# Expert loop in program order on four engines, memory rows loaded late, router logits partly inside the last projection

## The chip, the cores and the metric

The kernel runs on one core of one Trainium2 chip. The metric is the device time in microseconds (us) of one execution. Five instruction streams matter: PE (TensorE, matmuls and transposes), DVE (VectorE), ACT (ScalarE), POOL (GpSimd) and SP (SyncE, which issues nearly all loads and stores). Each runs its own instructions in the order in which they stand and stops at the first whose inputs are not there.

## What is computed

Two transformer blocks on 512 tokens of 1024 features, in fp32. The first block ends in a hierarchical mixture of experts, which is the part that the change touches:

```
x = x + einsum('bsd,de->bse', y, w_out)              # "last projection" of the first block: x1
h2 = rmsnorm(x, norm_ffn_g).reshape(b * s, d)
group_logits = h @ w_router_group + b                 # 8 groups
g_sel = argmax(group_logits)                          # one group for each token
in_group = (h @ w_router_expert + b)[its group]       # 4 experts
top_vals, top_idx = top_k(in_group, 2)                # two of them
for e in range(32):
    hid = silu(h @ w_gate[e]) * (h @ w_up[e])         # 1024 -> 256
    out = out + (hid @ w_down[e]) * combine[:, e]     # 256 -> 1024
```

The second block has two layers: A (dilated windows) and B, and in both the tokens also attend to a second input of 512 "memory" rows. The memory's keys and values for both layers need only those rows and weights, so the kernel computes them beside the experts and uses them as filling work for PE.

## The kernel before, in words

**Weights.** A `Stream` object (L195 on) loads all big weights in a planned order on SP, as far ahead as the buffer rings of its "lanes" allow. A tile of 128x1024 fp32 is 512 KB. Tiles of the lane "w" are split after landing into two fp32r parts, `whi` on ACT (L229) and `wlo` on DVE or, for every eighth, on POOL (L232), and used in products of three matmuls (L370 to L372). Expert weights are used as they land, without a split. Each call of `ws.get()` also pushes loads and splits ahead (`advance`), so splits of weights that come later in the plan are emitted wherever the loop happens to take an expert tile.

**Router.** After the last projection (L1120s), x1 is transposed (L1119), the logits are made with the router's weights as the stationary side, 64 columns by 512 tokens (L1160), copied out (`lT`) and turned back by four transposing matmuls (L1177). Then DVE picks group and experts, PE counts positions (L1242, `ppos`), DVE forms slot ranks, PE forms the slot table (L1338), and `v0i` holds, for each slot, the row to gather. Steps of the memory's keys and values (`pump(kv, n)`) fill PE in between.

**Experts.** The 32 experts are handled as 16 pairs, 64 slots for each of the two. For pair j, POOL gathers 128 rows of x1 from HBM with an indirect DMA into `xg` (L1377, two buffers), DVE scales them (L1380), PE transposes them in 8 steps (L1385), DVE copies them out (`xgt`, L1387); PE multiplies by gate and up in four units (L1400), ACT and DVE form the hidden values (L1405 to L1407), PE turns them (L1413), ACT copies (`hid`, L1415), PE multiplies by down (L1426), ACT and DVE copy `y` (L1430, L1428), and POOL scatters it to HBM by an indirect DMA (`yd`, L1431). The loop at L1462 stands in this order in the program:

```
for j in range(-1, 16):
    hidden(j); gate_up(j+1) units 0 to 2; tokens(j+2): gather and transposes
    turned(j); gate_up(j+1) unit 3; down(j) and scatter
```

A scheduler orders the instructions of each engine, except inside `tc.manual_schedule(engines=...)`, where the named engines keep the program's order. Before, only PE is named in the router and in the loop. At j == 8 the loop also loads the memory rows for layer B's values into `mem` and splits them (`mem_load`, L635 on ACT, L636 on DVE).

**After the loop.** `vB_steps` and `mem_k` (memory work of layer B and more) run on PE while SP reads `yd` back and DVE adds it to x2 (`add_experts`, L1553, L1554); squares for two norms follow, then the transposes and layer A's first projection.

Of the kernel before, what the change touches and what calls it, by code (L numbers as in the profile page):

```python
# [195 lines left out]
class Stream:  # L196
# [3 lines left out]
    def __init__(self, nc, plan, ahead):  # L200
        self.nc, self.plan, self.ahead = nc, plan, ahead
        self.lanes, self.count, self.raw, self.done, self.pos = {}, {}, [], [], 0
# [75 lines left out]
ROUTER = (1, 1, 1, 2, 4, 4, 8)  # L278
AFTER = (5, 3, 3, 3, 1)
# [30 lines left out]
def build(tc, A, out, dbg=None):  # L310
# [259 lines left out]
    plan2 = [(ap, "k" if 8 <= j < 12 else "w") for j, ap in enumerate(plan2)]  # L570
    ws = Stream(nc, [(ap, "w") for ap in plan1 + kv0] + moe_u + plan2, ahead=3)
    ws.lane("w", wp, "wraw", 3, "w", 5, pool_every=8)
    ws.lane("k", wp, "wraw", 3, "w", 5, pool_every=1)
# [31 lines left out]
    def outproj(yT, xs, view, after=None):  # L605
# [4 lines left out]
        for n in range(2):  # L610
            pp = [acc(), acc(), scp(), scp()]
            for u in range(nk // 2):
                hi, lo = ws.get()
                for c in range(4):
# [13 lines left out]
    def mem_load(pool):  # L628

        res = []  # L630
        for j in range(2):
            t = pool.tile([128, 1024], F32, name="mem", tag="mraw", bufs=MR)
            nc.sync.dma_start(t, mTd[:, 1024 * j:1024 * j + 1024])
# [456 lines left out]
    wr = big("wr", "y", 2)[:, :512].rearrange("p (k n) -> p k n", k=8)  # L1090
    G.memset(wr, 0.0)
    nc.sync.dma_start(wr[:, :, :40], A["w_r"])
    V.tensor_tensor(wr, wr, vec(V_FFN, 8)[:, :, None].to_broadcast([128, 8, 64]), OP.mult)
    ident2 = mo.tile([128, 40], F32, name="ident2")
    V.tensor_tensor(ident2, ident[:, :40], ident[:, 64:104], OP.add)
# [10 lines left out]

    def square_half(pool, junk):
# [34 lines left out]
    outproj(yT, x1, xv, after_x1)  # L1142
# [10 lines left out]
    order = ExitStack()  # L1153
    order.enter_context(tc.manual_schedule(engines={mybir.EngineType.PE}))
    plT = otp()

    def logits(k):
        for kk in (k, k + 1):
            q = slice(64 * (kk % 2), 64 * (kk % 2) + 64)
            T.matmul(plT[q], wr[:, kk, :], x1T[kk], start=kk < 2, stop=kk > 5)  # L1160
    logits(0)
    logits(2)
    x1_transpose(4)
    x1_transpose(5)
    pump(kv, ROUTER[0])
    x1_transpose(6)
    pump(kv, ROUTER[1])
    x1_transpose(7)
    logits(4)
    pump(kv, ROUTER[2])  # L1170
    logits(6)
    lT = mo.tile([128, 512], F32, name="lT", tag="mkn", bufs=2)
    V.tensor_copy(lT, plT)
    pump(kv, ROUTER[3])
    pl = otp()
    for c in range(4):
        T.matmul(pl[:, c * 40:c * 40 + 40], lT[:, c * 128:c * 128 + 128], ident2, start=True, stop=True)  # L1177
    pump(kv, ROUTER[4])

# [9 lines left out]
    def small(shape, name, dtype=F32, tag=None, rows=128):
        return mo.tile([rows] + shape, dtype, name=name, tag=tag or name)  # L1190

    def bc(ap, shape):
        return ap.to_broadcast([128] + shape)
# [19 lines left out]
    basei = [small([4, 5], "basei%d" % z, BF) for z in range(2)]  # L1213
    for z in range(2):
        for i in range(4):
            V.memset(basei[z][:, i, 0:1], float(4 * z + i + 1))
    iop = small([1], "iop")
    junkp = mo.tile([128, 512], F32, name="junkp", tag="mkn", bufs=2)[:, :128]
    V.scalar_tensor_tensor(junkp, ident, 1.0, iota, op0=OP.mult, op1=OP.mult, accum_out=iop)
    for z in range(2):  # L1220
        V.tensor_copy(basei[z][:, :, 1], iop.to_broadcast([128, 4]))
    revi = small([8], "revi")
    V.tensor_scalar(revi, iota[:, :8], -1.0, 8.0, OP.mult, OP.add)
# [9 lines left out]
    sel = [small([4, 8, 4], "sel%d" % z, BF) for z in range(2)]  # L1233
    for z, o in enumerate((o1, o2)):
        V.tensor_tensor(sel[z], bc(oh[:, :, :, None], [4, 8, 4]), bc(o[:, :, None, :], [4, 8, 4]), OP.mult)
    both = small([4, 32], "both", BF)
    flat = [z.rearrange("p c g e -> p c (g e)") for z in sel]
    V.tensor_tensor(both, flat[0], flat[1], OP.add)
    ppos = otp()
# [5 lines left out]
    pump(kv, ROUTER[5])  # L1245
# [54 lines left out]
    def three(dst, src, n):  # L1300
        for z in range(3):
            V.tensor_copy(dst[:, :, n * z:n * z + n], src)
            if z < 2:
                V.tensor_tensor(src, src, dst[:, :, n * z:n * z + n], OP.subtract)

    def payload(base, z, n, name):
        p = small([4, 32, n], name, BF)
        V.tensor_tensor(p, bc(base[:, :, None, :], [4, 32, n]), bc(flat[z][:, :, :, None], [4, 32, n]), OP.mult)
        return p

    r1 = small([4, 1], "r1")
    V.tensor_copy(r1[:, :, 0], r[:, :4])
    three(basei[0][:, :, 2:5], r1, 1)
    V.tensor_copy(basei[1][:, :, 2:5], basei[0][:, :, 2:5])
    payi = [payload(basei[z], z, 5, "payi%d" % z) for z in range(2)]

    def slot_ranks(shift, name):
# [3 lines left out]
        for z in range(2):  # L1321
# [5 lines left out]
            for i in range(4):  # L1327
                V.tensor_scalar(R[:, i, :], iota[:, :NS], pr[:, i:i + 1], None, OP.is_equal)
# [16 lines left out]
    def slot_rows(t, n, name):  # L1345
# [10 lines left out]
        V.tensor_tensor(ix, f, e, OP.add)  # L1356
        w = small([n], name + "w")
        V.tensor_tensor(w, t[:, :, 4], t[:, :, 3], OP.add)
        V.tensor_tensor(w, w, t[:, :, 2], OP.add)
        return ix, ox, w  # L1360

    def slot_weights(t, n, name):
# [3 lines left out]
        V.tensor_tensor(w, w, t[:, :, 0], OP.add)  # L1366
        return w

    ranks = slot_ranks(None, "s0")
    idx, odx, rw = slot_rows(slot_table(ranks, payi, 5, "ti"), 16, "v0")  # L1370
    pump(kv, ROUTER[6])
    order.close()

    def gather_tokens(j, ix, rms):
# [5 lines left out]
        V.tensor_scalar(xg, xg, rms, None, OP.mult)  # L1380
# [21 lines left out]
    def hidden(p, w):  # L1402

        th = hchunk("th")[:, :256]
        S.activation(th, p[:, :256], AF.Tanh, scale=0.5)  # L1405
# [30 lines left out]
    Xg = gather_tokens(0, idx[:, 0:1], rw[:, 0:1])  # L1436
    pump(kv, 32 - sum(ROUTER))
    basew = [small([4, 3], "basew%d" % z, BF) for z in range(2)]
    payw = []
    for z, w in enumerate(top_weights()):  # L1440
        three(basew[z], w[:, :, None], 1)
        payw.append(payload(basew[z], z, 3, "payw%d" % z))
    cw = slot_weights(slot_table(ranks, payw, 3, "tw"), 16, "cw")
    nx, ofs, next_i = counts()

# [7 lines left out]
    def tokens(j):  # L1453
        return gather_tokens(j, idx[:, j:j + 1], rw[:, j:j + 1])

    order = ExitStack()
    order.enter_context(tc.manual_schedule(engines={mybir.EngineType.PE}))
    pg, Xnext = acc(), None
    for j in range(-1, 16):
        if j >= 0:  # L1460
            th = hidden(pg, cw[:, j:j + 1])
# [26 lines left out]
    def extra(e):  # L1488
# [36 lines left out]
        down(get, turned(hidden(p, w[:, 0:1])), ox)  # L1525
# [14 lines left out]
    ET = mybir.EngineType  # L1540
    with tc.manual_schedule(engines={ET.PE, ET.Activation, ET.DVE, ET.Pool}):
        kmB = [mo.tile([128, 512], F32, name="kmB", tag="mraw", bufs=MR) for _ in range(2)]
        ms, ms2 = ([big("m", "mraw", MR) for c in range(4)] for _ in range(2))
        for c in range(4):
            nc.sync.dma_start(ms[c], yd[128 * c:128 * c + 128, :])
            nc.sync.dma_start(ms2[c], yd[512 + 128 * c:640 + 128 * c, :])
        pump(vB_steps)
# [3 lines left out]
        def add_experts(c):  # L1551
            pump(kv, AFTER[c])
            V.tensor_tensor(x2[c], x2[c], ms[c], OP.add)  # L1553
            V.tensor_tensor(x2[c], x2[c], ms2[c], OP.add)  # L1554
            tap("x2", x2[c], c)
            S.activation(ms[c], x2[c], AF.Square, accum_out=s3[:, c:c + 1])
        hT = transposed(x2, gFA, hp_, "h", 16, tps=tps, more=scp, before=add_experts)
        for c in range(4):
            m = ms[c]
# [501 lines left out]
```

## Time and profile before

| | us |
|---|---|
| median of 3 runs | 1874.06 |
| lowest, highest run | 1872.5, 1877.54 |
| profiled execution | 1873.42 |
| its span in the trace | 1871.6 |
| PE busy in it | 1791.2 (96%) |
| DVE, ACT, POOL busy | 894.3, 733.9, 368.0 |
| mean granted PE clock, as a share of full speed | 0.984 |

The span is what the trace covers; 1.8 us of the profiled execution lie around it. Times within the trace count from the span's start. The router takes the stretch from 447 to 489, the expert loop that from 489 to 741, and the work up to layer A's first projection that from 741 to 778. PE's busy share is an average over all stages.

### The profile page before, as it was taken

How to read it: one execution, taken by the hardware profiler on the slowest of the kernel's cores; microseconds unless marked ns; L12 is line 12 of the kernel's file. 1: busy time of each engine (PE TensorE's matmuls, PEld its weight loads, DVE VectorE, ACT ScalarE, POOL GpSimd, SP SyncE). 2: the span in 40 equal slices, each digit the busy share in tenths (PEclk: the TensorE clock that was granted, in tenths of full speed). 3: DMA queues.
4: the chain of work that ended last, by engine and by line, in shares of the span. 5: the costliest groups of instructions: out<-in, count | busy, mean ns of one | idle time of the engine just before them, and what ended most of it. 6: DMA issues, size and time to landing. Idle time of an engine off the chain costs nothing.

```text
span 1871.6 us, 25322 instructions
## 1 busy us (share of the span) xinstructions
PE 1791.2 (96%) x9426; PEld 1381.5 (74%) x9426; DVE 894.3 (48%) x1880; ACT 733.9 (39%) x1754; POOL 368.0 (20%) x463
## 2 busy tenths in 40 slices
PE   8999999998999578999999999999999999999999
PEld 8857776786533123799989899989888787777887
DVE  4389765276422221742342422342475326676571
ACT  5475355343100011544554433553564332333460
POOL 1301200010111011413514203514200002222200
PEclk9999999999999789999999999999999999999999
DMA  5221222178899998642211222212233322121231
GB/s 179 79 68 35 73 68 74 58 248 316 327 414 409 413 396 312 231 132 90 91 59 55 68 90 90 79 54 71 68 113 110 117 90 80 57 68 57 68 113 57
DMA packets 83684, 261.16 MB, mean 140 GB/s; under 512 B 12896, under 2 KB 14688, under 8 KB 83552
## 3 DMA queue, kind: packets, MB, share of 16 engines
q1 hardware_dynamic: 78080, 248.43, 37.6%
q0 software_dynamic: 4608, 8.40, 1.2%
q10 hardware_dynamic: 864, 2.62, 0.4%
q8 instruction: 77, 1.26, 0.3%
q14 instruction: 55, 0.45, 0.1%
HBM read 248.92 MB, written 18.87 MB: 143 GB/s over the span
## 4 chain that ended last, share of the span: by engine, by line
PE 85%; DMA 9%; DVE 3%; ACT 2%; issue 1%; SPq 0%; POOL 0%; POOLq 0%; ACTq 0%; DVEq 0%
PE acc L370 19%; PE acc L372 18%; PE acc L371 18%; PE acc L1400 3%; PE sc L370 3%; PE sc L371 3%; PE sc L372 3%; DMA mraw<-in_w_moe 3%; DMA hraw<-in_w_moe 2%; PE sc L1931 1%; PE sc L1426 1%; PE sc L911 1%; PE sc L1727 1%; DMA xraw<-in_w_moe 1%; PE tp L1668 1%; PE oT L936 1%
## 5 line engine op out<-in xcount | busy, mean ns | idle before, releaser
L370 PE MATMUL acc<-whi,hh 128*128 128x512 f32 (+2 forms) x936 | 382.5, 410 | 1.4 <-ACT hh L383 0.6
L371 PE MATMUL acc<-wlo,hh 128*128 128x512 f32 (+2 forms) x936 | 372.1, 398 | 0.0
L372 PE MATMUL acc<-whi,hl 128*128 128x512 f32 (+2 forms) x936 | 371.6, 399 | 0.0
L232 DVE TENSOR_TENSOR wlo<-wraw,whi 128x1024 fp32r<-128x1024 f32 (+4 forms) x209 | 244.6, 1174 | 254.0 <-ACT whi L229 253.3
L229 ACT ACTIVATE whi<-wraw 128x1024 fp32r<-128x1024 f32 (+4 forms) x239 | 239.2, 1002 | 294.2 <-PE acc L371 114.8
L370 PEld LDWEIGHTS acc<-whi,hh 128*128 128x128 f32 x936 | 223.1, 239 | 27.5 <-issue 2.8
L371 PEld LDWEIGHTS acc<-wlo,hh 128*128 128x128 f32 x936 | 223.8, 239 | 22.0 <-issue 1.7
L372 PEld LDWEIGHTS acc<-whi,hl 128*128 128x128 f32 x936 | 222.8, 239 | 21.5
L370 PE MATMUL acc<-hh,whi 128*128 128x512 f32 x448 | 184.7, 412 | 0.0
L372 PE MATMUL acc<-hh,wlo 128*128 128x512 f32 x448 | 177.7, 397 | 0.0
L371 PE MATMUL acc<-hl,whi 128*128 128x512 f32 x448 | 176.8, 395 | 0.0
L232 POOL TENSOR_TENSOR wlo<-wraw,whi 128x1024 fp32r<-128x1024 f32 (+3 forms) x30 | 69.1, 2304 | 514.9 <-ACT whi L229 423.9
L365 POOL TENSOR_TENSOR rs<-rsa,mhalf 128x4 f32<-128x4 f32 (+1 forms) x80 | 79.2, 990 | 333.2 <-DVE rsa L362 269.5
L707 ACT ACTIVATE hjk<-acc 128x128 bf16<-128x128 f32 x232 | 64.0, 276 | 106.6 <-PE acc L372 75.5
L370 PEld LDWEIGHTS acc<-hh,whi 128*128 128x128 f32 x448 | 84.5, 189 | 21.1 <-issue 4.9
L372 PEld LDWEIGHTS acc<-hh,wlo 128*128 128x128 f32 x448 | 84.2, 188 | 19.8 <-issue 1.0
L371 PEld LDWEIGHTS acc<-hl,whi 128*128 128x128 f32 x448 | 84.6, 189 | 15.5
L1400 PE MATMUL acc<-mraw,xgt 128*64 128x512 f32 x232 | 95.5, 621 | 0.3 <-DVE xgt L1387 0.3
L710 DVE TENSOR_TENSOR nat<-acc,rs 128x512 f32<-128x512 f32 x52 | 35.9, 691 | 61.2 <-POOL rs L365 43.4
L371 PE MATMUL sc<-wlo,hh 128*128 128x512 f32 (+2 forms) x144 | 56.0, 390 | 0.0
L370 PE MATMUL sc<-whi,hh 128*128 128x512 f32 (+2 forms) x144 | 55.7, 392 | 0.0
L372 PE MATMUL sc<-whi,hl 128*128 128x512 f32 (+2 forms) x144 | 55.0, 388 | 0.0
(546 smaller groups left out, 3084.7 us busy)
## 6 DMA issues: line engine op xcount, KB each, us to landing
mraw<-in_w_moe SPq DMA_DIRECT2D x86, 512.0 KB
wraw<-in_w_qka SPq DMA_DIRECT2D x48, 512.0 KB
xraw<-in_w_moe SPq DMA_DIRECT2D x25, 512.0 KB
hraw<-in_w_moe SPq DMA_DIRECT2D x44, 256.0 KB
praw<-in_w_moe SPq DMA_DIRECT2D x22, 512.0 KB
qraw<-in_w_moe SPq DMA_DIRECT2D x21, 512.0 KB
wraw<-in_w_va SPq DMA_DIRECT2D x20, 512.0 KB
wraw<-in_w_qfb SPq DMA_DIRECT2D x16, 512.0 KB
```

What stands on the lines that cost most here:

```text
L229: nc.scalar.activation(hi, raw, AF.Copy)
L232: eng.tensor_tensor(lo, raw, hi.bitcast(F32), OP.subtract)
L365: G.tensor_tensor(r[:, :m], t[:, :m], mhalf[:, :m], OP.pow)
L370: T.matmul(p, a[0], b[0], start=start, stop=False)
L371: T.matmul(p, a[0], b[1], start=False, stop=False)
L372: T.matmul(p, a[1], b[0], start=False, stop=stop)
L707: S.activation(jk, p[:, h * 128:h * 128 + 128], AF.Square, accum_out=st[:, h:h + 1])
L710: V.tensor_tensor(t.rearrange("p (h d) -> p h d", h=nh), p.rearrange("p (h d) -> p h d", h=nh), r[:, :nh, None].to_broadcast([128, nh, 128 ...
L911: T.matmul(pp[s][:, :W], a[:, i * 128:i * 128 + 128], b[:, :W], start=True, stop=True)
L936: T.matmul(o[64 * s:64 * s + 64, j * 128:512], vt[j][:, (2 * pr + s) * 64:(2 * pr + s) * 64 + 64], PT[pr, s][:, col[j]:col[j] + w], start= ...
L1400: T.matmul(p[z], X[2 * u + k][:, z], w[e][k], start=u + k == 0, stop=u + k == 4)
L1426: T.matmul(p[z], t[:, k * 128 + NS * e:k * 128 + NS * e + NS], w[e][k], start=k == 0, stop=k == 1)
```

## The change

1. **Router.** The logits are made with the transposed tokens as the stationary side, 128 tokens by 40 columns, in 32 matmuls (L1167 of the changed kernel) straight into the layout that DVE reads; `lT` and the four turning matmuls go. The half that needs only the first four transposed blocks stands inside the last unit of the last projection. DVE joins PE in keeping the program's order there. The payload products move from DVE to POOL, and four instructions for each slot rank become one. The filling steps are dealt out anew.
2. **Gathered rows** are no longer scaled by DVE; the norm's factor goes into the tanh's scale and the slot weights.
3. **Loop.** PE, ACT, DVE and POOL all keep the program's order, and a new limit `ws.upto` keeps splits of later weights out of it until j == 14.
4. **Memory rows** are loaded at j == 13 and split behind the loop (`mem_split`, L641, L642).
5. **After the loop** two of the adds stand between the memory steps, the second norm's square uses a precomputed gF squared, and one lane, which split four value weights on POOL alone, goes.

```diff
-            if not moved and d < i:
+            if not moved and d < i and (self.upto is None or d < self.upto):
...
-ROUTER = (1, 1, 1, 2, 4, 4, 8)
+ROUTER = (1, 1, 2, 9, 3)
...
-    plan2 = [(ap, "k" if 8 <= j < 12 else "w") for j, ap in enumerate(plan2)]
-    ws.lane("k", wp, "wraw", 3, "w", 5, pool_every=1)
...
+    def logits(k):
+        for kk in (k, k + 1):
+            for c in range(4):
+                T.matmul(pl[:, c * 40:c * 40 + 40], x1T[kk][:, run(c)], wr[:, kk, :], start=kk + c == 0,
+                         stop=kk == 7 and c == 3)
+    def early_logits():
+        logits(0)
+        logits(2)
+    outproj(yT, x1, xv, after_x1, early_logits)
...
-    for c in range(4):
-        T.matmul(pl[:, c * 40:c * 40 + 40], lT[:, c * 128:c * 128 + 128], ident2, start=True, stop=True)
...
-        V.tensor_scalar(xg, xg, rms, None, OP.mult)
...
-        S.activation(th, p[:, :256], AF.Tanh, scale=0.5)
+        S.activation(th, p[:, :256], AF.Tanh, scale=hr)
...
-    order.enter_context(tc.manual_schedule(engines={mybir.EngineType.PE}))
+    order.enter_context(tc.manual_schedule(engines={ET.PE, ET.Activation, ET.DVE, ET.Pool}))
+    own = len(plan1) + 8 + 192
+    ws.upto = own
...
-        if j == 8:
-            mT = mem_load(mo)
-            vB_steps = memory_steps(ws, mT, store_v, (scp, otp))
...
+        if j == 13:
+            mem2 = mem_load(mo)
+        if j == 14:
+            ws.upto = own + 2
...
+    mT = mem_split(mo, mem2)
+    ws.upto = own + 8
+    ws.advance()
     order.close()
+    vB_steps = memory_steps(ws, mT, store_v, (scp, otp))
...
-            (G if c < 1 else V).tensor_tensor(m, x2[c], gF, OP.mult)
-            S.activation(m, m, AF.Square, accum_out=s4[:, c:c + 1])
+            V.tensor_tensor_reduce(ms2[c], ms[c], gF2, 1.0, 0.0, OP.mult, OP.add, s4[:, c:c + 1])
```

POOL's instructions at the head of the expert loop, where `xg` rows are gathers, `yd` rows scatters, and the number behind `y` tells one pair's result from the next. Before:

```order
L1377 DMA xg1_3908<-x1d_75,v0i_4515 128x1024
L1377 DMA xg0_3907<-x1d_75,v0i_4515 128x1024
L1431 DMA yd_76<-y_4799,v0o_4516 1024x1024
L1377 DMA xg1_3908<-x1d_75,v0i_4515 128x1024
L1431 DMA yd_76<-y_4951,v0o_4516 1024x1024
```

And in the changed kernel:

```order
L1380 DMA xg0_3907<-x1d_75,v0i_4522 128x1024
L365 TENSOR_TENSOR rs_4623<-rsa_4622,mhalf_73 128x4
L365 TENSOR_TENSOR rs_4635<-rsa_4634,mhalf_73 128x4
L1433 DMA yd_76<-y_4807,v0o_4523 1024x1024
L1380 DMA xg1_3908<-x1d_75,v0i_4522 128x1024
L1433 DMA yd_76<-y_4958,v0o_4523 1024x1024
L1380 DMA xg0_3907<-x1d_75,v0i_4522 128x1024
```

Before, five gathers (of pairs 0 to 4) stand ahead of the first scatter. In the changed kernel three do; the gather of pair 3 stands behind the scatter of pair 0, that of pair 4 behind the scatter of pair 1, and so on, one scatter and one gather in turn, to the gather of pair 15 behind the scatter of pair 12.

ACT's instructions in the middle of the loop, where L635 splits the memory rows and L229 splits later weights. Before:

```order
L1430 ACTIVATE y<-sc 128x512
L635 ACTIVATE mT<-mem 128x1024 x2
L1415 ACTIVATE hid<-tp 128x256
L1405 ACTIVATE th<-acc 128x256
L1430 ACTIVATE y<-sc 128x512
L1415 ACTIVATE hid<-tp 128x256
L1405 ACTIVATE th<-acc 128x256
L1430 ACTIVATE y<-sc 128x512
L229 ACTIVATE whi<-wraw 128x1024
L1415 ACTIVATE hid<-tp 128x256
```

In the changed kernel, at the loop's end:

```order
L1417 ACTIVATE hid<-tp 128x256
L1432 ACTIVATE y<-sc 128x512
L1407 ACTIVATE th<-acc,v0w 128x256
L1417 ACTIVATE hid<-tp 128x256
L229 ACTIVATE whi<-wraw 128x1024 x2
L1432 ACTIVATE y<-sc 128x512
L641 ACTIVATE mT<-mem 128x1024 x2
L229 ACTIVATE whi<-wraw 128x1024 x3
L1543 COMPARE_AND_BRANCH
```

The split of the memory rows has left its place ahead of a `hid` copy in the middle of the loop and stands behind the last `y` copy; the splits of later weights stand in the last pass and behind it.

## Rows read from the trace of the kernel before

**Rows 1.** Waits of PE: engine, line, released by, total us, times, longest.

```profile
PE tp L1413 <- DVE xgt L1387: 35.5, 14, 21.4
PE oT L1242 <- DVE both L1238: 5.8, 1, 5.8
PE acc L1400 <- DMA xraw<-in_w_moe: 5.3, 1, 5.3
```

**Rows 2.** Timeline of ACT, 612 to 690: start, us, operation, idle time before it, releaser.

```profile
643.37 1.06 ACT L635 ACTIVATE mT<-mem 128x1024 fp32r<-128x1024 f32 x1 [28.78 <-DMA mem<-mTd]
...
681.34 1.06 ACT L229 ACTIVATE whi<-wraw 128x1024 fp32r<-128x1024 f32 x1 [15.01 <-DMA wraw<-in_w_mv]
```

**Rows 3.** Windows of 10 us: busy time by engine, then PE clock, DMA share, GB/s.

```profile
630.00:640.00 10.00, 0.00 (x0) 0.00 (x0) 0.00 (x0) 0.00 (x0) 0.11 (x1) 0.63 1.03 408
...
680.00:690.00 10.00, 5.03 (x14) 1.60 (x16) 3.33 (x5) 2.09 (x4) 0.00 (x0) 0.50 0.95 356
...
730.00:740.00 10.00, 7.35 (x22) 2.79 (x24) 0.69 (x1) 0.98 (x2) 0.97 (x1) 0.83 0.58 215
```

**Rows 4.** Timeline of PE, 597 to 612, one pass of the loop.

```profile
597.64 1.09 PE L1385 MATMUL tp<-c_ident,xg 128*128 128x128 f32 x8
...
604.65 0.59 PE L1400 MATMUL acc<-mraw,xgt 128*64 128x512 f32 x1
...
609.90 1.09 PE L1385 MATMUL tp<-c_ident,xg 128*128 128x128 f32 x8
```

**Rows 5.** Timeline of POOL, the same stretch.

```profile
599.00 1.02 POOL L1377 DMA_INDIRECT xg<-x1d,v0i  x1 [9.95 <-PE tp L1385]
600.33 1.02 POOL L1431 DMA_INDIRECT yd<-y,v0o  x1 [0.31 <-issue]
```

**Rows 6.** The tile view of `xg`: 16 gathers, from issue to landing.

```profile
DMA to landing us min/median/max: 6.7/7.2/8.3
```

**Rows 7.** The tile view of `yd`: 16 scatters and 8 loads back, the same.

```profile
DMA to landing us min/median/max: 3.2/7.2/8.5
```

**Rows 8.** Timeline of DVE and of POOL, end of the loop.

```profile
741.00 0.69 DVE L1428 COPY y<-sc 128x512 f32<-128x512 f32 x1 [8.00 <-PE sc L1426]
...
742.44 0.97 POOL L1431 DMA_INDIRECT yd<-y,v0o  x1 [4.84 <-DVE y L1428]
```

**Rows 9.** Timeline of PE, end of the loop.

```profile
734.95 4.39 PE L1426 MATMUL sc<-mraw,hid 128*64 128x512 f32 x9 [2.30 <-DMA mraw<-in_w_moe]
...
740.32 0.59 PE L1426 MATMUL sc<-hraw,hid 128*64 128x512 f32 x1
744.88 0.52 PE L370 MATMUL sc<-whi,mT 128*128 128x512 f32 x1 [3.96 <-DVEq L1532]
```

**Rows 10.** Windows of 1 us after three of PE's idle times, columns as in group 3.

```profile
468.00:469.00 1.00, 1.00 (x9) 0.81 (x5) 1.00 (x10) 0.00 (x0) 0.00 (x0) 0.50 0.20 82
...
522.00:523.00 1.00, 1.00 (x6) 0.29 (x4) 0.00 (x0) 0.00 (x0) 0.00 (x0) 0.50 1.06 424
523.00:524.00 1.00, 1.00 (x6) 0.18 (x2) 0.00 (x0) 0.00 (x0) 0.00 (x0) 0.85 1.03 418
...
747.00:748.00 1.00, 1.00 (x4) 0.81 (x3) 0.00 (x0) 0.00 (x0) 0.00 (x0) 0.50 0.02 8
748.00:749.00 1.00, 1.00 (x4) 0.77 (x4) 0.00 (x0) 0.00 (x0) 0.00 (x0) 0.71 0.00 0
```

**Rows 11.** Timeline of PE in the router and at the loop's start.

```profile
457.99 0.98 PE L1177 MATMUL oT<-ident,lT 128*128 128x40 f32 x8
...
467.62 0.18 PE L1242 MATMUL oT<-both,tri 128*128 128x32 bf16 x1 [5.78 <-DVE both L1238]
...
489.06 5.37 PE L1400 MATMUL acc<-mraw,xgt 128*64 128x512 f32 x24 [0.35 <-DVE xgt L1387]
```

**Rows 12.** Timeline of DVE: the first scaling of gathered rows; the last add.

```profile
483.73 0.76 DVE L1380 TENSOR_SCALAR xg<-xg,v0w 128x1024 f32<-128x1024 f32 x1 [5.38 <-DMA xg<-x1d,v0i]
...
768.01 3.31 DVE L1554 TENSOR_TENSOR x<-x,m 128x1024 f32<-128x1024 f32 x1
```

More of the change, by code (lines that the diff above doesn't have):

```diff
@@ L603, in swap_rope, with outproj @@
         eng.tensor_tensor(dst, a, b, OP.add)
-    def outproj(yT, xs, view, after=None):
+    def outproj(yT, xs, view, after=None, late=None):
         nk = len(yT)
@@ L613, in outproj @@
                 hi, lo = ws.get()
+                if late and n == 1 and u == nk // 2 - 1:
+                    late()
                 for c in range(4):
@@ L631, in mem_load, with mem_split @@
         for j in range(2):
-            t = pool.tile([128, 1024], F32, name="mem", tag="mraw", bufs=MR)
-            nc.sync.dma_start(t, mTd[:, 1024 * j:1024 * j + 1024])
+            res.append(pool.tile([128, 1024], F32, name="mem", tag="mraw", bufs=MR))
+            nc.sync.dma_start(res[j], mTd[:, 1024 * j:1024 * j + 1024])
+        return res
+    def mem_split(pool, raw):
+        res = []
+        for t in raw:
             hi, lo = (pool.tile([128, 1024], F32R, name="mT", tag="mT", bufs=4) for _ in range(2))
@@ L1105, in build, with small, bc @@
     G.memset(ones, 1.0)
+    def small(shape, name, dtype=F32, tag=None, rows=128):
+        return mo.tile([rows] + shape, dtype, name=name, tag=tag or name)
+    def bc(ap, shape):
+        return ap.to_broadcast([128] + shape)
+    basei = [small([4, 5], "basei%d" % z, BF) for z in range(2)]
+    for z in range(2):
+        for i in range(4):
+            V.memset(basei[z][:, i, 0:1], float(4 * z + i + 1))
+    iop = small([1], "iop")
+    junkp = mo.tile([128, 512], F32, name="junkp", tag="mkn", bufs=2)[:, :128]
+    V.scalar_tensor_tensor(junkp, ident, 1.0, iota, op0=OP.mult, op1=OP.mult, accum_out=iop)
+    for z in range(2):
+        V.tensor_copy(basei[z][:, :, 1], iop.to_broadcast([128, 4]))
+    revi = small([8], "revi")
+    V.tensor_scalar(revi, iota[:, :8], -1.0, 8.0, OP.mult, OP.add)
     def square_half(pool, junk):
@@ L1184, in half_sums, with three @@
         return s4
-    r = rsq(mo, half_sums(mo), 1024)
+    order = ExitStack()
+    order.enter_context(tc.manual_schedule(engines={mybir.EngineType.PE, mybir.EngineType.DVE}))
+    ws.upto = len(plan1) + 5
+    x1_transpose(4)
+    x1_transpose(5)
+    pump(kv, ROUTER[0])
+    x1_transpose(6)
+    x1_transpose(7)
+    pump(kv, ROUTER[1])
+    logits(4)
+    r = rsq(mo, half_sums(mo), 1024)
+    logits(6)
+    def three(dst, src, n):
+        for z in range(3):
+            V.tensor_copy(dst[:, :, n * z:n * z + n], src)
+            if z < 2:
+                V.tensor_tensor(src, src, dst[:, :, n * z:n * z + n], OP.subtract)
+    r1 = small([4, 1], "r1")
+    V.tensor_copy(r1[:, :, 0], r[:, :4])
+    three(basei[0][:, :, 2:5], r1, 1)
+    V.tensor_copy(basei[1][:, :, 2:5], basei[0][:, :, 2:5])
+    pump(kv, ROUTER[2])
     ws.lane("x", xp, "xn", 4)
[L1189 to L1193, printed above, removed]
     L = small([4, 40], "lg")
@@ L1211, in first_max @@
         return m, e
[L1213 to L1223, printed above, removed]
     gm, oh = first_max(gl, 8, "g")
@@ L1233, in build, with payload @@
     sel = [small([4, 8, 4], "sel%d" % z, BF) for z in range(2)]
+    flat = [z.rearrange("p c g e -> p c (g e)") for z in sel]
+    def payload(base, z, n, name):
+        p = small([4, 32, n], name, BF)
+        G.tensor_tensor(p, bc(base[:, :, None, :], [4, 32, n]), bc(flat[z][:, :, :, None], [4, 32, n]), OP.mult)
+        return p
+    payi = []
     for z, o in enumerate((o1, o2)):
         V.tensor_tensor(sel[z], bc(oh[:, :, :, None], [4, 8, 4]), bc(o[:, :, None, :], [4, 8, 4]), OP.mult)
+        payi.append(payload(basei[z], z, 5, "payi%d" % z))
     both = small([4, 32], "both", BF)
-    flat = [z.rearrange("p c g e -> p c (g e)") for z in sel]
     V.tensor_tensor(both, flat[0], flat[1], OP.add)
+    pump(kv, ROUTER[3])
     ppos = otp()
@@ L1296, in top_weights @@
         return wgp, e2
[L1300 to L1315, printed above, removed]
     def slot_ranks(shift, name):
@@ L1326, in slot_ranks @@
             R = small([4, NS], name + "R", BF, "slotR%d" % z)
-            for i in range(4):
-                V.tensor_scalar(R[:, i, :], iota[:, :NS], pr[:, i:i + 1], None, OP.is_equal)
+            V.tensor_tensor(R, bc(iota[:, None, :NS], [4, NS]), bc(pr[:, :, None], [4, NS]), OP.is_equal)
             res.append(R)
@@ L1355, in slot_rows @@
         V.tensor_scalar(e, f, 511.5, -512.0, OP.is_ge, OP.mult)
-        V.tensor_tensor(ix, f, e, OP.add)
+        last["rows"] = V.tensor_tensor(ix, f, e, OP.add).ins
         w = small([n], name + "w")
@@ L1366, in slot_weights, with gather_tokens @@
         V.tensor_tensor(w, w, t[:, :, 0], OP.add)
+        for _ in range(2):
+            V.scalar_tensor_tensor(w, hr, 2.0, w, op0=OP.mult, op1=OP.mult)
         return w
     ranks = slot_ranks(None, "s0")
+    cntm = small([32], "cntm")
+    V.tensor_scalar(cntm, ppos[:, 128:160], -1.0, None, OP.add)
     idx, odx, rw = slot_rows(slot_table(ranks, payi, 5, "ti"), 16, "v0")
-    pump(kv, ROUTER[6])
     order.close()
-    def gather_tokens(j, ix, rms):
+    ws.upto = None
+    def gather_tokens(j, ix):
         xg = xgs[j % 2]
@@ L1435, in build @@
     V.tensor_tensor(gFA, vec(V_FIN, 8), vec(V_A, 8), OP.mult)
[L1436 to L1444, printed above, removed]
+    with tc.issue_after(last["rows"]):
+        Xg = gather_tokens(0, idx[:, 0:1])
+        pump(kv, 32 - sum(ROUTER))
+        basew = [small([4, 3], "basew%d" % z, BF) for z in range(2)]
+        payw = []
+        for z, w in enumerate(top_weights()):
+            three(basew[z], w[:, :, None], 1)
+            payw.append(payload(basew[z], z, 3, "payw%d" % z))
+        cw = slot_weights(slot_table(ranks, payw, 3, "tw"), rw, 16, "cw")
+        nx, ofs, next_i = counts()
     def store_v(c, p):
@@ L1453, in tokens @@
     def tokens(j):
-        return gather_tokens(j, idx[:, j:j + 1], rw[:, j:j + 1])
+        return gather_tokens(j, idx[:, j:j + 1])
     order = ExitStack()
-    order.enter_context(tc.manual_schedule(engines={mybir.EngineType.PE}))
+    ET = mybir.EngineType
+    order.enter_context(tc.manual_schedule(engines={ET.PE, ET.Activation, ET.DVE, ET.Pool}))
+    own = len(plan1) + 8 + 192
+    ws.upto = own
     pg, Xnext = acc(), None
@@ L1524, in extra @@
         gate_up(get, X, p, range(4))
-        down(get, turned(hidden(p, w[:, 0:1])), ox)
+        down(get, turned(hidden(p, hr[:, 0:1], w[:, 0:1])), ox)
     if not dbg.get("noif"):
@@ L1549, in build, with beside @@
         tps = [bank() for bank in (scp, scp, scp, otp, tpp, tpp)]
[L1551 to L1557, printed above, removed]
+        def beside(c):
+            if c != 1:
+                pump(kv, AFTER[c + 2])
+            if c in (0, 2):
+                add_experts(2 + c // 2)
+            if c == 3:
+                ws.upto = own + 10
+                ws.advance()
+        hT = transposed(x2, gFA, hp_, "h", 16, tps=tps, more=scp, before=beside)
+        ws.upto = None
+        for c in range(1, 4):
+            square(c)
         for c in range(4):
-            m = ms[c]
-            (G if c < 1 else V).tensor_tensor(m, x2[c], gF, OP.mult)
-            S.activation(m, m, AF.Square, accum_out=s4[:, c:c + 1])
+            V.tensor_tensor_reduce(ms2[c], ms[c], gF2, 1.0, 0.0, OP.mult, OP.add, s4[:, c:c + 1])
         V.tensor_scalar(a12[:, 1], s3, 1.0 / 1024, EPS, OP.mult, OP.add)
```

74 lines of the change are left out of this document (30 added, 44 removed).

## The prediction

> **What bounds the kernel now.** I read the page's busy shares first, then the waits of PE, then the stretch of the expert loop in windows and timelines, and last the order of the instructions. PE is busy 96% of the span, so in most stages only less PE work could shorten the kernel. The change touches the one stretch where that isn't so. The waits of PE [rows 1] show it: 35.5 us are spent at the turning of the hidden values, 21.4 of them in one piece, 5.8 at the positions of the router and 5.3 at a gate tile.
>
> The long piece is a wait in ACT's queue. The split of the memory rows stands ahead of a `hid` copy and waits 28.78 us for its data; later a split of a value weight waits 15.01 us in the same manner [rows 2]. In the windows PE does nothing from 630 to 640 and half its share from 680 to 690 [rows 3]. But the last columns there matter as much: with PE standing still the DMA engines move 408 GB/s, and only in the second stall do they fall to 356. The weights keep coming while PE waits, and PE uses them up afterwards. So removing a stall of PE is worth only what the DMA had lost or will lose.
>
> **The loop by its work.** One pass at full clock lasts 609.90 - 597.64 = 12.26 us from transposes to transposes [rows 4]. Thirteen passes of that kind (j = 1 to 13) make 159.4. The others, costed by the same rows, are j = -1 without down 8.7, j = 0 12.3, j = 14 without transposes 10.8 and j = 15 with down alone 3.9: 35.7. Together 195.1 us. From 489.06 [rows 11] to the last down matmul at 740.9 [rows 9] the loop took 251.8; the other 56.7 are the stalls, waits for weights and half clock.
>
> **What the DMA allows.** A pass uses 12 tiles of 512 KB; at 408 GB/s that is 15.4 us, and 16.7 with one more tile's worth for gather and scatter (an estimate from their sizes). More than a pass of work, so the DMA sets a floor. The last gate of it is the wait of 2.30 us for the last down tile at 734.95 [rows 9]. In SP's new order five tiles fewer stand ahead of it (eight value and key weights before, three now), 6.4 us, and the dip of the second stall, about 2 us. If the loop begins 4 us earlier, as below, the weights do too. That puts the floor of the loop's end at about 728, 13 us before today's.
>
> **Part by part.** *Router.* The copy and the turning matmuls, 0.98 us for these with a copy and two hand-overs around them [rows 11], leave the chain; payloads and slot ranks lose some 2 us of DVE time; PE's idle time of 5.78 us, with the half clock behind it [rows 10, 11], is filled with memory steps. The scale of the gathered rows, 0.76 us [rows 12], goes. What PE must do before the positions stays, now with 32 small logit matmuls (estimated at 0.2 us each from the 0.98 us for four of the nearest shape), so it is late next. Sum: the loop starts at 484.9, 4.2 us earlier; the ends are 0, if PE's steps eat all of it, and 7, PE's idle time and the half-clock cost together.
>
> *Scaling* off the loop's DVE gives nothing there: a gather is issued behind the transposes that free its buffer [rows 5], lands 7.2 us later [rows 6], and its turn is almost two passes away. That cover goes with the next point.
>
> *Loop order.* This decides. In the changed kernel POOL issues the gather of pair j+3 behind the scatter of pair j, and that scatter waits for the copies of `y` behind the last down matmul of pair j. Count from that matmul's end. The copy starts 0.1 us later and takes 0.69, POOL starts the scatter 0.75 after that, 0.97 [rows 8], then 0.31 to the next DMA [rows 5]: the gather is issued 2.8 us after the down product ended. It lands 6.7 to 8.3 us later [rows 6], at 9.5 to 11.1. PE, however, is ready to transpose it after three units of gate and up, which is 609.90 - 604.65 = 5.25 us [rows 4]. So PE waits 4.3 to 5.9 us in each of the 13 passes. Queued behind the transposes on PE are `turned`, the fourth unit and down, so nothing covers it. I take 4.3, the short end, because in longer passes the DMA queue has less in it.
>
> The Trainium skill ("DMA: Bandwidth & Descriptors", the section on the anatomy of one DMA on the SWDGE path) fits such a transfer as 2.0 us plus the bytes over 436 KB a microsecond. By it 512 KB would land in 3.2 us and PE would wait 0.8; the gathers of this trace took more than twice that, and the measured time stands in the sum.
>
> *Clock.* Each idle time of 2.3 us or more in this trace is followed by half clock (0.50, 1.2 of 2.4 GHz): after the 5.78 us [rows 10, 11], the 5.3 [rows 1, 10], the 3.96 [rows 9, 10] and even the 2.30 (its window reads 0.83 [rows 3, 9]), and in both long stalls [rows 3]. After the 3.96 us PE ran 3.1 us at half, which costs 1.5 us; after the 5.3 us it ran 5.3, which costs 2.65. I take 1.75 per pass, nearer to the short one, as the wait is nearer to 3.96 than to 5.3 by the shorter landing; the ends are 0 and 2.65.
>
> *Memory rows, splits.* The two stalls go (35.5 us, less 14 waits of 0.35). That gain is inside the floor and the 195.1 and isn't counted twice.
>
> *Behind the loop* ACT and DVE must first split the memory rows and later weights: PE's first memory step comes some 9 us after the last down matmul instead of 3.96 [rows 9]. The adds gain: no POOL split runs beside them, where the last one took 3.31 us [rows 12] and the others 1.2. Before, the adds ended the stretch; now PE's own 32 memory steps do. I count +1, between -3 and +4.
>
> **Sum.** 484.9 + 195.1 + 13 x (4.3 + 1.75) = 758.7 for the loop's end, 17.8 later than 740.9, and 1 behind it: +18.8. On the profiled execution's 1873.42, which lies 0.6 below the median, that is 1892 us. A difference under 0.3% (5.6 us) can't be told from none here.
>
> **The rivals.**
> *The floor decides, as the order intends (faster).* If the passes fit into 15.95 us (728 - 520.6 over 13), wait and clock cost together under 3.7, only the DMA counts: 1873.4 - 13 + 1 = about 1862. The gathers would have to land within 6.1 us and the clock to stay full. For it: the shortest landing in [rows 7] is 3.2 us, and by that the wait would be 0.8; the skill's fit says the same. Against: all 16 gathers took 6.7 or more, beside the weight stream at 408 GB/s, and PE's freed tiles keep that stream running while the gather is under way. Chance 0.14.
> *The clock stays full.* The waits come, but 4.3 to 4.8 us leave no half clock: 680 + 13 x 4.3 to 4.8 = 736 to 742, so 1869 to 1876, within 0.3%. Against it stand all six idle times. Chance 0.11.
> *Every pass pays in full.* Landing at 7.2 us (a wait of 4.8) and 2.65 of clock: 680 + 13 x 7.4 = 776.6, +36.7, 1910. For it: the median landing; against: with passes of 19.7 us the DMA has 3 us to spare in each. Chance 0.14.
> *The gain of the late split is lost behind the loop* (a new wait of 9 us or more for the memory rows, splits or value weights ahead of PE's first step): another 5 on top of any case; it moves the middle case to 1897 and no sign. It is inside the 0.61 of my forecast.
>
> **How the numbers follow.** My forecast, slower by some clock cost in most passes (1880 to 1903), 0.61; full price 0.14; full clock 0.11, nearly all of it within 0.3%; floor 0.14, nearly all faster. That makes slower 0.75, same 0.10, faster 0.15. The range goes from the floor's 1862 to just short of the full price, 1908. The forecast's own range is 1880 to 1903.
>
> **What would show it.** In the waits of PE a line for transposes waiting on the gather (DMA of `xg`), about 13 times, 4 to 5 us each, takes the place of the 35.5. POOL's timeline shows scatter and gather 1.3 us apart, the gather second. The clock in the loop's windows reads 0.7 to 0.9 instead of 1.00, and the DMA moves less than 400 GB/s there. The loop starts near 485 and ends near 759; the 5.78 at the positions is gone. It is wrong if the transposes wait under 2 us per pass, if the DMA stays at 408 GB/s throughout the loop, or if the loop ends before 740.

## The result, and the profile after

| | before | after |
|---|---|---|
| median, us (runs) | 1874.37 (4) | 1917.67 (4) |
| lowest to highest | 1872.5 to 1877.54 | 1917.2 to 1918.47 |
| profiled execution | 1873.42 | 1918.47 |
| its span | 1871.6 | 1916.7 |

The ratio is 1.023, with a 95% interval of 1.0212 to 1.0247: slower, as forecast, but by 43 us instead of 18, and above the range. The waits of PE after (engine, line, released by, total us, times, longest) answer to [rows 1]:

```profile
PE tp L1387 <- DMA xg<-x1d,v0i: 77.4, 12, 7.3
PE sc L370 <- ACTq L1543: 6.6, 1, 6.6
...
PE acc L1402 <- DMA xraw<-in_w_moe: 3.1, 1, 3.1
```

The 35.5 us at the hidden values and the 5.8 at the positions are gone. In their place PE waits 12 times at the transposes for the gathered rows, 6.45 us in the mean. One pass of the loop in the timeline of POOL (start, us, operation, idle time before it):

```profile
566.89 1.01 POOL L1433 DMA_INDIRECT yd<-y,v0o  x1 [18.77 <-DVE th L1408]
568.21 1.02 POOL L1380 DMA_INDIRECT xg<-x1d,v0i  x1 [0.31 <-issue]
```

and of PE, where L1428 is the down product and L1387 the transposes:

```profile
564.75 0.59 PE L1428 MATMUL sc<-mraw,hid 128*64 128x512 f32 x1
...
569.90 0.59 PE L1402 MATMUL acc<-mraw,xgt 128*64 128x512 f32 x1
576.14 1.94 PE L1387 MATMUL tp<-c_ident,xg 128*128 128x128 f32 x8 [5.65 <-DMA xg<-x1d,v0i]
578.02 0.69 PE L1415 MATMUL tp<-c_ident,th 128*128 128x128 f32 x2
```

The gather is issued 2.87 us after the down product's end (565.34), and the transposes start 7.93 later. Over the twelve passes that wait, the gather is issued 2.85 to 2.87 after the down product, and the transposes start 7.73 to 9.59 after that, 8.74 in the mean. The tile view of `xg` says the same of the landing, against 6.7/7.2/8.3 before [rows 6]:

```profile
DMA to landing us min/median/max: 6.8/8.3/9.5
```

The windows of 1 us around that pass (columns as in [rows 3]) show the clock and the DMA:

```profile
571.00:572.00 1.00, 0.00 (x0) 0.00 (x0) 0.00 (x0) 0.00 (x0) 0.00 (x0) 1.00 1.00 389
572.00:573.00 1.00, 0.00 (x0) 0.00 (x0) 0.00 (x0) 0.00 (x0) 0.00 (x0) 1.00 1.05 426
...
575.00:576.00 1.00, 0.00 (x0) 0.00 (x0) 0.00 (x0) 0.00 (x0) 0.00 (x0) 0.50 1.07 426
576.00:577.00 1.00, 0.86 (x4) 0.89 (x5) 0.00 (x0) 0.00 (x0) 0.00 (x0) 0.50 1.02 418
...
580.00:581.00 1.00, 1.00 (x4) 0.24 (x2) 0.00 (x0) 0.00 (x0) 0.00 (x0) 0.50 0.55 217
581.00:582.00 1.00, 1.00 (x6) 0.35 (x4) 0.00 (x0) 0.00 (x0) 0.00 (x0) 0.68 0.07 20
582.00:583.00 1.00, 1.00 (x8) 0.30 (x6) 0.00 (x0) 0.00 (x0) 0.00 (x0) 1.00 0.01 4
...
584.00:585.00 1.00, 1.00 (x8) 0.39 (x6) 0.00 (x0) 0.85 (x2) 0.00 (x0) 1.00 1.00 410
```

While PE stands still and the gather is under way (570.5 to 576.1), the DMA engines move 389 to 426 GB/s in every window of 1 us: the weights' rings, the buffers into which SP loads them, are being filled. They stand almost idle from 581 to 583.5, 5 us after the gather landed. The rings are full then: what SP waits for in the loop, 540 to 760, before it can issue the next load is mostly a tile that PE has not yet used.

```profile
SPq L217 <- PE acc L1402: 121.7, 42, 12.1
```

In this pass the clock falls to half 1.3 us before the end of the wait and is back 5.5 us after it; over the twelve passes these are 0.8 to 3.4 and 3.4 to 6.0.

Where the 45.1 us of span between the two profiles lie, by the starts of the same instruction in both:

| point in the program | before | after | difference |
|---|---|---|---|
| first gate and up product | 489.06 | 485.22 | -3.8 |
| end of the last down product | 740.9 | 787.5 | +46.5 |
| transposes of the first norm in layer A (L432) | 794.30 | 841.35 | +47.05 |
| end of the span | 1871.6 | 1916.7 | +45.1 |

All of the loss is in the loop: 302.2 us instead of 251.8.

```profile
786.86 0.59 PE L1428 MATMUL sc<-hraw,hid 128*64 128x512 f32 x1
794.03 0.79 PE L370 MATMUL sc<-whi,mT 128*128 128x512 f32 x1 [6.58 <-ACTq L1543]
```

### The profile page after: what moved, and what is told of

The parts are those of the page before. It is cut to its first block, busy times and chain, and to the rows that moved or that the text cites. A ratio compares the mean times of both kernels' runs of the same rounds, so it can differ in the third digit from the quotient of the medians.

```text
span 1916.7 us, 25383 instructions
## 1 busy us (share of the span) xinstructions
PE 1803.1 (94%) x9466; PEld 1394.1 (73%) x9466; DVE 882.8 (46%) x1864; ACT 730.7 (38%) x1747; POOL 358.9 (19%) x461
## 4 chain that ended last, share of the span: by engine, by line
PE 55%; DVE 2%; ACT 1%; POOL 0%; issue 0%; DMA 0%; ACTq 0%; POOLq 0%; DVEq 0%
PE acc L370 13%; PE acc L371 13%; PE acc L372 13%; PE sc L370 2%; PE sc L371 2%; PE sc L372 2%; PE sc L1958 1%; PE sc L1754 1%; PE tp L1695 1%; PE sc L1757 1%; PE tp L1762 1%; PE oT L1771 1%; PE oT L2006 1%; DVE wlo L232 1%; ACT whi L229 0%; PE oT L1766 0%
## 5 line engine op out<-in xcount | busy, mean ns | idle before, releaser
L232 DVE TENSOR_TENSOR wlo<-wraw,whi 128x1024 fp32r<-128x1024 f32 (+4 forms) x213 | 249.2, 1176 | 228.5 <-ACT whi L229 227.7
L229 ACT ACTIVATE whi<-wraw 128x1024 fp32r<-128x1024 f32 (+4 forms) x243 | 243.3, 1003 | 264.2 <-PE acc L371 113.1
L1402 PE MATMUL acc<-mraw,xgt 128*64 128x512 f32 x232 | 102.4, 654 | 0.0
L1387 PE MATMUL tp<-c_ident,xg 128*128 128x128 f32 x128 | 27.6, 387 | 77.4 <-DMA xg<-x1d,v0i 77.4
L1389 DVE TENSOR_TENSOR xgt<-tp,c_vecs 128x512 f32<-128x512 f32 x32 | 21.8, 690 | 152.5 <-PE tp L1387 106.7
L1387 PEld LDWEIGHTS tp<-c_ident,xg 128*128 128x128 f32 x128 | 22.3, 203 | 90.2 <-issue 89.2
L1417 ACT ACTIVATE hid<-tp 128x256 f32<-128x256 f32 x16 | 6.1, 383 | 204.0 <-PE tp L1415 204.0
```

The lines of the kernel that those rows point to most:

```text
L229: nc.scalar.activation(hi, raw, AF.Copy)
L232: eng.tensor_tensor(lo, raw, hi.bitcast(F32), OP.subtract)
L1387: T.transpose(tp[:, k * 128:k * 128 + 128], xg[:, (4 * q + k) * 128:(4 * q + k) * 128 + 128], ident)
L1389: V.tensor_tensor(t.rearrange("p (k n) -> p k n", k=4), tp.rearrange("p (k n) -> p k n", k=4), vec(V_FFN + 4 * q, 4)[:, :, None].to_broadc ...
L1402: T.matmul(p[z], X[2 * u + k][:, z], w[e][k], start=u + k == 0, stop=u + k == 4)
```

## The experiments

All are made from the changed kernel unless it is said. A build whose order is changed in one place also gets another order from the scheduler in places where no order is forced, and the part behind L432 came out between 1074.3 and 1080.2 us in the twelve profiles. So the loop is read by its own end, and total times only to within 10 us or so.

**1. The gather issued as soon as its buffer is free.**

```diff
     def tokens(j):
-        return gather_tokens(j, idx[:, j:j + 1])
+        X = gather_tokens(j, idx[:, j:j + 1], j >= FIRST)
+        if FIRST <= j + 2 < 16:
+            gather(j + 2, idx[:, j + 2:j + 3])
+        return X
...
+    FIRST = 1
+    gather(1, idx[:, 1:2])
+    gather(2, idx[:, 2:3])
```

> The changed kernel with one move: each gather is issued as soon as the transposes have freed its buffer, ahead of the scatters, as the kernel before had it. Theory 1 (the gather behind the scatter is the whole loss): no transposes wait for a gather, the clock in the loop is back at 1.00, the loop ends at the floor of the weights, 728 to 735, and the time is 1858 to 1866 us. Rival (the order of ACT and DVE, or the rows loaded late, lose time of their own): the waits of PE move to another line and the time stays above 1885.

`gather` issues the indirect DMA alone, and the new last argument keeps `gather_tokens` from issuing it again.

Measured: 1860.79 us (5 runs, 1859.37 to 1864.66), ratio to the kernel before 0.9939 [0.9918, 0.9959]. No wait of the transposes for a gather is left; what PE waits for in the loop are mostly weights (the third line stands behind the loop):

```profile
PE acc L1406 <- DMA hraw<-in_w_moe: 7.2, 3, 4.6
PE sc L1432 <- DMA hraw<-in_w_moe: 6.2, 2, 4.5
PE sc L370 <- DVEq L1553: 6.1, 1, 6.1
PE acc L1406 <- DMA xraw<-in_w_moe: 6.0, 2, 5.8
```

and the loop ends at 730.5:

```profile
729.95 0.59 PE L1432 MATMUL sc<-hraw,hid 128*64 128x512 f32 x1
736.69 0.77 PE L370 MATMUL sc<-whi,mT 128*128 128x512 f32 x1 [6.15 <-DVEq L1553]
```

That is within 2.5 us of the floor of 728 that the prediction worked out from the weights, and the 1862 of its first rival. With this one move the changed kernel is 0.6% faster than the kernel before, and its loop ends 10.4 us earlier; of all kernels tried it has the lowest median, and those of experiments 2 and 8 lie within its spread.

**2. POOL left to the scheduler.** `ET.Pool` is taken out of the loop's list of engines.

> The changed kernel with POOL taken out of the engines that keep the program's order in the loop; PE, ACT and DVE stay in order. Its gathers then stand ahead of the scatters in POOL's queue again. Theory 1 (POOL's place for the gather is the whole loss): as with the gathers issued early, 1857 to 1866 us. Rival (some later gather still ends up behind a scatter that waits): single waits of 4 to 7 us, 1866 to 1885.

Measured: 1862.59 us, ratio 0.9938 [0.9923, 0.9954]. The scheduler puts the gathers ahead of the scatters by itself; no line of PE's waits names `xg`. Theory 1 again, and by other means.

**3. The kernel before with POOL alone in program order.**

```diff
-    order.enter_context(tc.manual_schedule(engines={mybir.EngineType.PE}))
+    order.enter_context(tc.manual_schedule(engines={mybir.EngineType.PE, mybir.EngineType.Pool}))
```

> The kernel before with POOL alone added to the engines that keep the program's order in the loop; nothing else of the change. Theory 1: its gathers stand behind the scatters too, waits of 6 to 7 us for the gathered rows and half clock in most passes; the stall at the memory rows shrinks but stays: 1915 to 1945 us. Rival (POOL's order alone does nothing, it needs ACT and DVE in order as well): 1870 to 1880.

Measured: 1933.57 us, ratio 1.0315 [1.0289, 1.0341]. Nothing else of the change is in it:

```profile
PE tp L1385 <- DVE xg L1380: 89.5, 12, 8.3
PE oT L1242 <- DVE both L1238: 5.8, 1, 5.8
```

The wait of 7.5 us in each pass is 1.0 larger here, 0.8 of it by the scaling on DVE between landing and transposes. The stall at the memory rows, which I expected to shrink but stay, is gone from PE's waits. So POOL's place for the gather is enough for the loss, and (with 1 and 2) without it there is no loss.

**4. The gather ahead of the scatter, but still behind y.**

```diff
+        if nxt:
+            G.tensor_copy(small([2], "ysee"), y[:, 511:513])
+            gather(nxt, idx[:, nxt:nxt + 1])
         nc.gpsimd.indirect_dma_start(out=yd, out_offset=bass.IndirectOffsetOnAxis(ap=ox, axis=0),
```

> The changed kernel, gather still issued only after y is complete (a copy of two columns of y on POOL keeps that wait), but ahead of the pair's scatter instead of behind it. It is issued 1.0 us earlier (2.0 instead of 3.0 after the down product). Theory a (the scatter just ahead in the same queue makes the landing 8.3 instead of 7.2): landing near 7.0, waits of 4.1 instead of 6.4, 1885 to 1895 us. Theory b (the weights' loads issued at that moment make it): landing stays 8 to 8.5, waits 5.4, 1900 to 1908.

Measured: 1901.81 us (1896.39 to 1905.18), ratio 1.0158 [1.0131, 1.0185]; the profiled execution, the fastest of the four, took 1896.39 and its loop ends at 763.2, 24.3 earlier than in the changed kernel.

```profile
PE tp L1391 <- DMA xg<-x1d,v0i: 50.9, 12, 4.9
```

```profile
DMA to landing us min/median/max: 6.0/7.4/8.6
```

In the twelve passes that wait, the gather is issued 1.73 to 2.06 us after the down product, 1.1 earlier, and its transposes follow 7.61 us later in the mean instead of 8.74. The wait is 4.24. By landing and wait this is theory a: with no scatter issued ahead of it a gather lands some 1.1 us sooner, and of the 6.45 us of wait 1.1 are the time to issue the scatter and 1.1 its share of the landing. The median, though, lies above the 1885 to 1895 that was expected of theory a and within theory b's 1900 to 1908. So the trace speaks for the scatter, the time doesn't decide, and that the loads of weights have a part in the landing too isn't ruled out.

**5. PE kept busy during the wait.**

```diff
+            if q == 0 and warm:
+                for _ in range(46):
+                    T.transpose(tp[:, :128], ident, ident)
```

> The changed kernel with 46 idle transposes of the identity (about 6 us at full clock) on PE ahead of the transposes of pairs 3 to 15, so that PE isn't idle while the gather is under way; nothing else moves. Theory 1 (of some 9 us lost per pass 6.4 are the wait and 2.6 the half clock behind it): clock near 1.00 in the loop, 13 x 2.6 = 34 us less, 1880 to 1890 us. Rival (the half clock costs little since the next wait takes up what it loses): 1905 to 1918.

Measured: 1909.79 us, ratio 1.0197 [1.0168, 1.0226]: the rival's time, but little of its reason. The clock did what was wanted: 1.00 in 20 of the 22 windows of 10 us from 540 to 760 (570 to 580 below, where the changed kernel reads 0.74).

```profile
570.00:580.00 10.00, 10.00 (x70) 6.45 (x66) 1.35 (x3) 0.00 (x0) 2.03 (x2) 1.00 0.98 357
```

From the start of the transposes to the end of the down product a pass takes 7.18 us here (ten of eleven passes) and 8.95 in the changed kernel (mean of the eleven), so half clock costs 1.8 us in each, not the 2.6 that I had put into the expectation. The twelve passes with a wait last 19.04 us in the mean instead of 20.40, 1.36 of the 1.8 each and 16 less in all, but the pass ahead of them, the first with idle transposes, took 26.3 us instead of 18.2. Its rows had landed long before, so the 5.24 us of idle transposes filled no wait and came on top:

```profile
520.11 5.24 PE L1388 MATMUL tp<-c_ident 128*128 128x128 f32 x46
```

The rest is a longer wait for the `xraw` tile there, 4.65 instead of 3.07, with half clock behind it. The loop ends at 781.0, 6.5 earlier.

**6. One pass more of lead, still behind a scatter.**

```diff
             down(ws.get, t, odx[:, j:j + 1])
+            if j < 12:
+                gather(j + 4, idx[:, j + 4:j + 5])
```

> The changed kernel, each gather still right behind a scatter on POOL, but that of pair j+4 behind the scatter of pair j instead of j+3: one whole pass more of lead, with the same two buffers and the same order of scatter and gather. Theory 1 (not the neighbourhood of the scatter but the missing lead loses the time; the neighbourhood only lengthens the landing): landing 8 to 9 us as in the changed kernel, no wait at the transposes, 1859 to 1863 us. Rival (scatter and gather in turn on POOL slow the loop by themselves): 1870 or more.

Measured: 1872.61 us, ratio 0.9995 [0.9986, 1.0005]. The time is the rival's, the loop is theory 1's: no transposes wait, seven passes in a row take the full-clock 12.26 us, and the rows are there over 6 us before PE wants them, although they land later than in experiment 1 (6.6/7.0/7.5):

```profile
DMA to landing us min/median/max: 7.2/7.9/8.5
```

The 11 us above experiment 1 are 4.1 at the loop's end, which waits 4.99 us for the last down tile, 1.7 up to L432 and 4.9 behind it, where the two kernels differ only by what the scheduler made of them.

```profile
731.27 1.08 PE L1432 MATMUL sc<-mraw,hid 128*64 128x512 f32 x1 [4.99 <-DMA mraw<-in_w_moe]
```

Whether the turn of scatter and gather has a part in the 4.1 stays open.

**7. The memory rows early again, gathers early.** The load and the split go back to j == 8.

> Gathers early, and the memory rows loaded and split at j == 8 again, ahead of a hid copy on ACT. Theory 1 (the loop is bound by the weights' transfers, and a stall of PE is caught up from tiles that land meanwhile): PE waits some 15 to 25 us at one place again, and the loop ends only 0 to 8 us later than with the rows late: 1860 to 1870. Rival (the stall is lost time, so its removal was worth 20 us or more): 1880 or more.

Measured: 1873.06 us, ratio to before 0.9996 [0.9987, 1.0006]. PE stalls for 37.6 us in one piece, since ACT waits for the rows (its timeline):

```profile
639.99 1.06 ACT L641 ACTIVATE mT<-mem 128x1024 fp32r<-128x1024 f32 x1 [38.91 <-DMA mem<-mTd]
```

Yet the loop ends at 738.2, only 7.7 us later than with the rows late. The total is 12 later, 3 more than theory 1 allowed and 7 below the rival's 1880; 4 of the 12 lie behind L432. So of a stall of 37.6 us some 30 are made up from weights that land in the meantime: from 606 to 646 the DMA engines move 391 GB/s.

**8. The loop's start held back by 4 us, gathers early.** 34 idle transposes (3.93 us) stand ahead of the first product.

> Gathers early, and 34 idle transposes on PE, about 4 us, ahead of the loop's first product, which takes back what the router part gained. Theory 1 (the loop's end is set by the weights; the rings are full at its start, so their stream begins when PE frees the first tile): the end moves by the 4 us, 1863 to 1867. Rival (the stream runs on by itself and takes the late start up): end and time unchanged, 1859 to 1862.

Measured: 1861.22 us, ratio 0.9933 [0.9918, 0.9949]; the loop starts at 488.42 and ends at 728.5. The rival is right, but the test is smaller than was meant: the scheduler's other order brought the idle transposes forward, so the start is only 2.4 us later than in experiment 1 (486.03). The stream of weights doesn't wait for the first product: it runs at 418 GB/s from 480 on.

```profile
480.00:490.00 10.00, 10.00 (x80) 7.89 (x80) 4.47 (x16) 2.94 (x16) 3.09 (x3) 1.00 1.03 418
```

```profile
488.42 5.37 PE L1406 MATMUL acc<-mraw,xgt 128*64 128x512 f32 x24
```

A start 2.4 us later therefore costs nothing here. That all of the 3.8 us that the router part gains are worth nothing is likely by this, but not shown.

**9. x2 loaded behind the experts' weights, gathers early.** A column of each x2 tile is written on POOL at j == 14, so that its load stands behind.

> Gathers early, and the four tiles of x2 (512 KB each, needed only for the adds behind the loop) are loaded behind the last expert weights instead of among them. Theory 1 (weights bind the loop's end): it ends 4 x 1.28 = 5 us earlier; of that up to 4 us may go again since a value weight is now loaded behind three of these tiles: 1855 to 1860. Rival (something else sets the end, or the value weight's delay takes it all): 1860 to 1864.

Measured: 1867.32 us, ratio 0.9959 [0.9946, 0.9973]: faster than before, slower than experiment 1, and neither theory's. The loop ends at 729.2, only 1.4 earlier than there. In experiment 1 only two of the four loads, issued at 697.1 and 702.1, stood ahead of the tile for which PE waits last, until 714.8; the others were issued at 712.9 and 715.4. Two tiles are 2.6 us, and that last wait ends 1.8 us earlier here. Then PE waits 10.4 us instead of 6.1 at its first memory step, since ACT must split a value and a key weight first and both now land behind the moved tiles:

```profile
PE sc L370 <- ACTq L1555: 10.4, 1, 10.4
```

```profile
735.00 1.06 ACT L229 ACTIVATE whi<-wraw 128x1024 fp32r<-128x1024 f32 x1 [3.99 <-DMA wraw<-in_w_mv]
738.37 1.06 ACT L229 ACTIVATE whi<-wraw 128x1024 fp32r<-128x1024 f32 x1 [2.32 <-DMA wraw<-in_w_mk]
```

**10. Two splits moved behind the branch, gathers early.** `ws.upto = own + 8` and the `advance` stand ahead of `pump(vB_steps)`, behind the branch, instead of right behind the loop.

> Gathers early, and two of the splits of value weights that stand on DVE (2.35 us) and ACT ahead of the branch behind the loop are moved behind that branch. Theory 1 (PE's 6.1 us of idle time there end with DVE's last split ahead of the branch): PE starts 2 us earlier, 1857 to 1860. Rival (the branch waits for SP and the memory rows, or the moved splits are late for the third memory step): no change or slower, 1860 to 1864.

Measured: 1872.7 us, ratio 0.9995 [0.9986, 1.0004]. PE's idle time there fell only from 6.1 to 5.7, and 5.3 us of a new wait for the adds came behind it; the scheduler's other order also started the loop 2.4 later. The time is neither theory's, a miss.

```profile
PE sc L370 <- DVEq L1551: 5.7, 1, 5.7
PE sc L404 <- DVE x L1569: 5.3, 1, 5.3
```

## Why the prediction was wrong

**Right.** The mechanism: the gather stands behind the scatter, which waits for the down product; the line of waits that was named appeared, 12 times for about 13; the gather's issue, 2.8 forecast, came 2.86 after the down product; the loop's start, 484.9, came at 485.2; the stretch behind the loop, +1, came at +0.5 (PE's first memory step came 6.6 us after the loop, not 9). The floor of 728 was reached to within 2.5 us, at 730.5, once the gathers were early. The DMA moved 308 GB/s in the loop, 540 to 760, where under 400 was named as a sign.

**Right by luck.** The clock's 1.75 us per pass measured 1.8. It was set between 1.5 and 2.65, nearer to 1.5, because the wait was to be near 3.96 us. The wait was 6.45, and by that reasoning the cost should have been above 2.65. It did not grow with the wait: in experiment 4, with waits of 4.24, the same stretch of a pass took 8.85 us against 7.18 (eleven passes), 1.7 more. Nor does the length of an idle time alone tell whether half clock follows, as the prediction read from its trace: in the changed kernel the wait of 3.07 us that ends at 511.80 left the clock at 1.00 (window below), and in experiment 1 a wait of 2.05 us that ends at 136.92 was followed by 0.50 from 138 on. The 3.1 us of half clock that the prediction put behind the 3.96 are 3.4 by the windows from 745 to 749 (0.58, 0.50, 0.50, 0.71).

```profile
510.00:520.00 10.00, 7.43 (x32) 2.77 (x34) 1.29 (x2) 0.38 (x1) 0.00 (x0) 1.00 1.04 410
```

**Wrong: one term.** "So PE waits 4.3 to 5.9 us in each of the 13 passes ... I take 4.3, the short end, because in longer passes the DMA queue has less in it." The step that failed is the landing inside this wait: 6.7 us was taken, 8.3 was the most that was allowed, and in the twelve passes the rows landed 8.6 us after the issue in the mean. So the wait was 6.45, above even the long end. Two things are in that. The reason for the short end is false: the longer pass does leave the DMA idle, but 5 us after the landing, not during it. While PE waits for the gather the rings that it has just emptied are being filled at 389 to 426 GB/s. And both ends came from gathers that had no transfer of POOL's own just ahead [rows 5, 6]; behind a scatter the gather takes 1.1 us more by experiment 4, and 0.9 by the medians of experiments 6 and 1 (7.9 against 7.0). What adds the few tenths that are left of the 8.6 isn't shown.

With the measured 6.45 and 1.8 the prediction's own sum gives 485.2 + 195.1 + 13 x (6.45 + 1.8) = 787.6 against 787.5. It fits that well because two smaller errors cancel: the first of the thirteen passes waited for a gate tile instead and lost 5.95 us and not 8.25, and the last pass took 6.2 us, not the 3.9 of "down alone", since PE first waits 1.6 us there for the hidden values and turns them.

**The range.** "Full price" put the long end of the half clock, 2.65, on top of a wait of 4.8 (by its own terms 776.2, not 776.6). The clock never cost that (2.4 at most in a pass), and the wait, which no row bounded with a scatter ahead, had no room upwards. An end of a range that is taken from rows of another arrangement is not an end.

**The rivals.** That the floor decides was given 0.14; it was the change's outcome but for the place of one instruction. For it to hold with the gather in that place the landing would have had to stay under 6.1 us; the shortest of the 16 took 6.8, and in ten of the twelve profiles no gather took under 6.3 (the shortest of experiment 4 took 6.0, that of experiment 3 5.1). The Trainium skill ("DMA: Bandwidth & Descriptors", anatomy of one DMA on the SWDGE path) gives 3.2 us for these 512 KB, an estimate by its fit; beside the stream of weights the medians measured here are 7.0 to 8.7, and these decide. That the clock stays full fell too: it read 0.50 in the transposes behind all 12 waits.

**What the late rows brought.** The forecast counted nothing for the stall that goes, since the floor holds it. Experiment 7 bears that out for the most part: 37.6 us of stall, 7.7 at the loop's end.

## What to carry to other kernels

When an engine is made to keep the program's order, look at what it starts that must land later: an engine that both fetches for the next steps and stores for the last one has to be told to fetch first, or the program's order puts each fetch behind the end of the step before. Price the landing by rows that have the same traffic at the same moment, and if there are none, give the term room on both sides. And ask of every stall what the transfers do meanwhile: here 30 of 37 us of PE's stall cost nothing, and a start 2.4 us later cost nothing, beside a stream of weights at about 410 GB/s.

## What the runs showed of the hardware

An indirect gather of 512 KB landed in 7.0 to 7.4 us (medians of eight profiles) beside the stream of weights when no scatter was issued just ahead, and in 7.9 to 8.7 (four profiles) where most gathers had one 1.3 us ahead. In experiment 5, where PE had idle transposes in front of each wait and 0.9 to 2.3 us of idle time were left, the clock stayed at 1.00 in most windows; after waits of 5.4 to 7.3 us in the changed kernel it read 0.50 in all twelve passes when the transposes ran (1.94 us instead of 1.09).
